# Stick-breaking attention: four query blocks meet the values in one group of products, in six of eight heads

## The chip, the cores and the metric

One core of a Trainium2 chip runs the whole program. The metric is the time of one execution on the device in microseconds (us); each kernel is run several times, and the median counts.

## The reference

A residual block over 1024 tokens of width 1024. Stick-breaking attention with 8 heads of width 64 and an HGRN2 recurrence run side by side on the same normalised input, are gated and merged, and an MLP and a last norm follow. The change is in the attention, which is:

```python
def block(args):
    qi, i = args                      # one block of 128 queries
    qpos = i * Q_BLOCK + jnp.arange(Q_BLOCK)
    z = jnp.einsum('bhqd,bhkd->bhqk', qi, k) * scale
    mask = kpos[None, :] < qpos[:, None]
    log_beta = jax.nn.log_sigmoid(z)
    log_rem = jnp.where(mask, log_beta - z, 0.0)
    between = lax.cumsum(log_rem, axis=3, reverse=True) - log_rem
    w = jnp.where(mask, jnp.exp(log_beta + between), 0.0)
    return jnp.einsum('bhqk,bhkd->bhqd', w, v)
```

A query sees only earlier keys: query block qb needs the key blocks 0 to qb.

## The kernel before

Products run on TensorE (PE) with operands split into a high part and a low remainder (`fp32r` tiles named ...h and ...l), so one exact product is two or three matmuls. `hi_lo` makes such a pair: ACT casts the high part out of the source (line 156), DVE subtracts it from the source for the low part (line 161). All matmuls go through the helper at line 128, all transposes through line 131.

In the attention stage (about 75 to 330 us of the span) the loop at the end of the kernel walks over 64 items, 8 heads times the query blocks in the order 7, 0, 6, 1, 5, 2, 4, 3. At each item it issues

- `weights` for the next item: DVE turns sigmoids into weights by a scan (`rm`, line 826) and a product (`bt`, line 169);
- `scores` for the item after that: PE forms z, ACT takes two sigmoids of each piece (`rm` line 804, `bt` line 807), POOL zeroes one column (line 808);
- some steps of the stream `st`, projections of later heads (`pjqk`, `pjf`, `pjq`, `pga`), which fill TensorE between the attention's own products;
- `turn` for the item itself: PE transposes its weight blocks into a PSUM bank `pw`, and `hi_lo` writes them as `wTh` and `wTl`;
- `values` for a pair of query blocks (2 qc, 2 qc + 1) whose both turns are done: PE multiplies the stationary values by the transposed weights into a bank `po`, ACT copies it to `osb` (line 902), and after a head's last copy two DMAs add its halves and store it. A pair that is complete at one item is multiplied at the next; the last pair of a head falls into the turn of the next head's block 7, between its two groups of transposes.

Products and filling are kept in order on TensorE by hand: `open_block` names the lane, and each block waits in issue order for its lane's last one, a filling block also for an earlier one of the main lane. `after` gives such an order without a wait.

A pair qc has 2 qc + 2 key blocks, each with 256 query columns; where key block 2 qc + 1 meets query block 2 qc there is nothing, and POOL sets those 128 columns to zero (line 862). Tiles come from a pool of 40 slots of 1024 columns (`slot`) and one of 10 halves of 512 columns (`slot_n` up to 512). The weights of pair 0 take two halves, those of pair 1 two slots, of pair 2 two slots and two halves, of pair 3 four slots. `to_come` counts a head's output copies.

Of the kernel before, what the change touches and what calls it, by code (L numbers as in the profile page):

```python
# [9 lines left out]
F32 = mybir.dt.float32  # L10
F32R = mybir.dt.float32r
# [8 lines left out]
P = 128  # L20
T = 1024
D = 1024
NT = T // P
# [16 lines left out]
def kernel(  # L40
# [19 lines left out]
    nc = tc.nc  # L60
# [14 lines left out]
    def slot(name, dt=F32):  # L75
        return spool.tile([P, 1024], dt, tag="s", name=name)

    def slot_n(name, n, dt=F32):

        if n <= 512:  # L80
            return hpool.tile([P, 512], dt, tag="h", name=name)
        return slot(name, dt)

    def bank(name):
        return psum.tile([P, 512], F32, tag="p", name=name)
# [19 lines left out]
    def after(ins, earlier):  # L105
        if earlier is not None and earlier.ins is not ins.ins:
            tc.add_manual_dep(ins.ins, earlier.ins.name, NOSYNC, reason="issue order")
        return ins

    def open_block(name):  # L110
        cur[0] = name
        lane = lanes[name]
        lane.gates = (lane.last,)
        if name == "main":
            lane.ends.append(lane.last)
        else:
            ends = lanes["main"].ends
            lane.gates += tuple(ends[-AHEAD : len(ends) - AHEAD + 1])

    def pe(ins):  # L120
        lane = lanes[cur[0]]
        for g in lane.gates:
            after(ins, g)
        lane.last = ins
        return ins

    def matmul(*a, **k):
        return pe(nc.tensor.matmul(*a, **k))  # L128

    def transpose(dst, src):  # L130
        return pe(nc.tensor.transpose(dst, src, ident))  # L131
# [9 lines left out]
    def lo_now(behind=None):  # L141
        while owed_wlo:
            after(owed_wlo.pop()(), behind)
# [9 lines left out]
    hi_behind, hi_last, turn_hi = [None], [None], [None]  # L153

    def hi_copy(dst, src):
        hi_last[0] = after(in_turn("act", nc.scalar.copy(dst, src)), hi_behind[0])  # L156

    def lo_sub(dst, src, hi):
        return in_turn(
            "dve",  # L160
            nc.vector.tensor_tensor(out=dst, in0=src, in1=hi.bitcast(F32), op=ALU.subtract),  # L161
        )

    def hi_lo(h, l, src):
        hi_copy(h, src)
        return lo_sub(l, src, h)
# [501 lines left out]
    vt, qk, osb = {}, {}, {}  # L668
# [9 lines left out]
    def v_stat(h, tb):  # L678
        c = ((tb % 2) * 4 + h % 4) * P
        return vt[h // 4, tb // 2][:, c : c + P]  # L680
# [101 lines left out]
    zs, wTt, seen = {}, {}, {}  # L782
    lastsel, turn_lo = [None], [None]
# [32 lines left out]
    def weights(h, qb):  # L816
# [7 lines left out]
        for i, (a, b) in enumerate(parts):  # L824
# [14 lines left out]
            if qb == 5:  # L839
                after(m, turn_lo[0])  # L840

    def turn(h, qb, between):

        open_block("main")
        bt, rm = zs.pop((h, qb))
        qc, par = qb // 2, qb % 2
        nkb = 2 * qc + 2
        if (h, qc) not in wTt:
            wTt[h, qc] = [
                tuple(  # L850
                    slot_n(f"wT{n}{h}_{qc}_{k0}", 256 * min(nkb - k0, 4), F32R).rearrange(
                        "p (k q) -> p k q", q=256
                    )
                    for n in "hl"
                )
                for k0 in range(0, nkb, 4)
            ]
        tiles = wTt[h, qc]
        qs = slice(par * P, (par + 1) * P)
        if par == 0:  # L860
            for t in tiles[-1]:
                after(nc.gpsimd.memset(t[:, (nkb - 1) % 4, qs].bitcast(F32), 0.0), lastsel[0])
        order = list(enumerate(tiles))
        for i, (th, tl) in order[::-1] if qb == NT - 1 else order:
            n = min(qb + 1 - 4 * i, 4)
            if n <= 0:
                continue
            if qb == NT - 1 and i == 0:
                between()
                open_block("main")  # L870
            pw = bank(f"pw{h}_{qb}_{i}")
            for kb in range(n):
                s0 = (4 * i + kb) * P
                transpose(pw[:, kb * P : (kb + 1) * P], bt[:, s0 : s0 + P])
            turn_lo[0] = hi_lo(
                th[:, 0:n, qs], tl[:, 0:n, qs], pw[:, : n * P].rearrange("p (k q) -> p k q", q=P)
            )
            turn_hi[0] = hi_last[0]
        lo_now(turn_lo[0])
        seen[h, qc] = seen.get((h, qc), 0) + 1  # L880
        return (h, qc) if seen[h, qc] == 2 else None

    to_come, od = {}, {}

    def values(h, qc):
        open_block("main")
        tiles = wTt.pop((h, qc))
        nkb = 2 * qc + 2
        po = bank(f"po{h}_{qc}")[:, 0:256]
        for kb in range(nkb):  # L890
            for i in range(2):
                matmul(
                    po,
                    v_stat(h, kb),
                    tiles[kb // 4][i][:, kb % 4, :],
                    start=kb == 0 and i == 0,
                    stop=kb == nkb - 1 and i == 1,
                )
        if to_come.get(h) is None:
            to_come[h] = NT // 2  # L900
            osb[h] = slot(f"osb{h}")
        kept = nc.scalar.copy(osb[h][:, qc * 256 : (qc + 1) * 256], po)
        to_come[h] -= 1
        keep_attended(behind=kept)
        if to_come[h] == 0:
            nc.gpsimd.dma_start(osb[h][0:DHS, :], osb[h][DHS:P, :], accum_op=ALU.add)
            summed.append(h)
# [3 lines left out]
    def keep_attended(queue=nc.scalar, behind=None):  # L911
        while summed:
            h = summed.pop()
            pair, r = h // 2, (h % 2) * DHS
            if r == 0:
                od[pair] = dram(f"od{pair}", [P, 1024])
            after(queue.dma_start(od[pair][r : r + DHS, :], osb.pop(h)[0:DHS, :]), behind)
# [1435 lines left out]
    for i, it in enumerate(items):  # L2353
        if i + 1 < len(items):
            weights(*items[i + 1])
        if i + 2 < len(items):
            st.finish(j_qk[items[min(i + 4, len(items) - 1)][0]])
            scores(*items[i + 2])
        if i % 2 == 1:
            next(wsums, None)  # L2360
        want = n_first + (i + 1) * (n_fill - n_first) // len(items)
        st.advance(want - done, j_att)
        done = want
        before = ready.popleft() if ready else None

        def between():
            if before:
                values(*before)

        r = turn(*it, between)  # L2370
        if i == len(items) - 2:
            attended[0] = turn_lo[0]
        if it[1] != NT - 1:
            between()
        if r:
            ready.append(r)
    st.finish(j_att)
    st.advance(1, j_q[2])
    while ready:
        values(*ready.popleft())  # L2380
# [125 lines left out]
```

## Time and profile before

| | |
|---|---|
| median of 3 runs | 1421.49 us (1421.34 to 1421.5) |
| profiled execution | 1421.23 us, its span 1419.4 us |
| granted TensorE clock | 0.999 |
| instructions | 18788 |
| value products (`po`) | 320, all of 256 columns |
| casts of transposed weights (`wTh`) | 96 |

The span is what the profiler saw between the first and the last instruction. "Busy" of TensorE counts overlapping, pipelined matmuls once. In the rows of groups, the numbers behind the bar are the busy time, the mean ns of one, and the idle time of the engine ahead of them with what ended it. In rows by time the first number is the start, the second the length, both in us.

### The profile page before, as it was taken

The page shows a single profiled execution, that of the slowest core. Times are in us where ns is not written, and L with a number is a line of the kernel's source. Part 1 is how long each engine was busy: PE and PEld are TensorE (multiplying, and loading weights), DVE is VectorE, ACT ScalarE, POOL GpSimd, SP SyncE. Part 2 cuts the span into 40 slices and gives each one's busy share as a digit, 9 for nine tenths or more (in the row PEclk, how much of TensorE's full clock was granted, in tenths as well). Part 3 has the DMA queues.
Part 4 walks back from the last instruction along what each step waited for, and adds up shares of the span by engine and source line. Part 5 has one row for each costly group of instructions (what it writes and reads, how often), then busy time and mean ns, then how long its engine had stood idle before and what let it go on. Part 6 is the DMA issues. An engine that isn't in the chain of part 4 may idle for free.

```text
span 1419.4 us, 18788 instructions
## 1 busy us (share of the span) xinstructions
PE 1408.7 (99%) x6848; PEld 1183.7 (83%) x6848; DVE 1087.5 (77%) x1494; ACT 684.5 (48%) x1181; POOL 142.0 (10%) x340
## 2 busy tenths in 40 slices
PE   9999999999999999999999999999999999999998
PEld 8888888888888888888888888888888888888886
DVE  7579988988567888887788897677666657768765
ACT  6356676664243554433244764445444443434343
POOL 3012223210011031000000300000000000000031
PEclk9999999999999999999999999999999999999999
DMA  7124445535135785364585515444446974776824
GB/s 239 29 67 127 104 101 96 106 78 151 65 73 163 233 219 178 130 215 156 158 300 194 185 53 171 163 162 141 140 145 239 354 263 153 279 273 234 281 100 180
DMA packets 162597, 237.72 MB, mean 167 GB/s; under 512 B 26268, under 2 KB 93384, under 8 KB 162504
## 3 DMA queue, kind: packets, MB, share of 16 engines
q1 hardware_dynamic: 145480, 190.37, 40.0%
q0 software_dynamic: 11584, 34.61, 9.9%
q10 hardware_dynamic: 5440, 11.54, 2.3%
q8 instruction: 54, 0.88, 0.2%
q14 instruction: 39, 0.32, 0.1%
HBM read 168.32 MB, written 66.06 MB: 165 GB/s over the span
## 4 chain that ended last, share of the span: by engine, by line
PE 97%; ACT 1%; DVE 1%; POOL 0%; DMA 0%; issue 0%; SPq 0%; DVEq 0%; ACTq 0%
PE pm L128 21%; PE pX L128 9%; PE pW L128 6%; PE pY L128 6%; PE pjqk L128 6%; PE pga L128 4%; PE gX L128 4%; PE gY L128 4%; PE pjf L128 3%; PE pys L128 3%; PE pji L128 3%; PE pyh L128 3%; PE pjq L128 3%; PE pjv L128 3%; PE po L128 3%; PE z L128 2%
## 5 line engine op out<-in xcount | busy, mean ns | idle before, releaser
L156 ACT CAST whid<-w 128x1024 fp32r<-128x1024 f32 x30 | 31.6, 1054 | 154.3 <-PE pm L128 86.0
L826 DVE TENSOR_TENSOR_SCAN rm<-rm,bits 128x511 f32<-128x511 f32 (+7 forms) x72 | 87.4, 1219 | 17.1 <-ACT rm L804 16.8
L128 PE MATMUL pm<-whid,sh 128*128 128x512 f32 x240 | 93.4, 389 | 0.0
L128 PE MATMUL pm<-wlod,sh 128*128 128x512 f32 x240 | 93.4, 389 | 0.0
L128 PE MATMUL pm<-whid,sl 128*128 128x512 f32 x240 | 93.4, 389 | 0.0
L128 PE MATMUL pm<-tl,sh 128*128 128x512 f32 (+1 forms) x210 | 81.3, 387 | 0.0
L128 PE MATMUL pm<-th,sl 128*128 128x512 f32 (+1 forms) x210 | 81.3, 387 | 0.0
L128 PE MATMUL pm<-th,sh 128*128 128x512 f32 (+1 forms) x210 | 81.3, 387 | 0.0
L161 DVE TENSOR_TENSOR wlod<-w,whid 128x1024 fp32r<-128x1024 f32 x30 | 36.6, 1222 | 55.7 <-ACT whid L156 55.7
L161 DVE TENSOR_TENSOR sl<-sa,sh 128x1024 fp32r<-128x1024 f32 x56 | 68.2, 1217 | 0.1
L156 ACT CAST wTh<-pw 128x512 fp32r<-128x512 f32 (+2 forms) x96 | 43.8, 485 | 41.6 <-PE pw L131 40.7
L156 ACT CAST sh<-sa 128x1024 fp32r<-128x1024 f32 x56 | 57.2, 1046 | 7.3 <-DMA sa<-ad 7.3
L2140 POOL TENSOR_SCALAR fss<-fss 128x1 f32<-128x1 f32 x8 | 3.3, 415 | 562.0 <-ACT fsc L2135 561.5
L161 DVE TENSOR_TENSOR wTl<-pw,wTh 128x512 fp32r<-128x512 f32 (+2 forms) x96 | 49.9, 546 | 4.3 <-ACT wTh L156 4.1
L128 PEld LDWEIGHTS pm<-whid,sl 128*128 128x128 f32 x240 | 45.1, 188 | 9.4
L128 PEld LDWEIGHTS pm<-wlod,sh 128*128 128x128 f32 x240 | 45.0, 187 | 9.4
L128 PEld LDWEIGHTS pm<-whid,sh 128*128 128x128 f32 x240 | 45.1, 188 | 9.3
L169 DVE TENSOR_TENSOR bt<-bt,rm 128x511 f32<-128x511 f32 (+7 forms) x72 | 49.0, 684 | 3.4
L804 ACT ACTIVATE rm<-z 128x511 f32<-128x511 f32 (+4 forms) x96 | 48.0, 500 | 5.5 <-PE z L128 2.9
L128 PE MATMUL pX<-sqh,t1l 128*128 128x512 f32 x128 | 49.9, 390 | 0.0
L128 PE MATMUL pX<-sql,t1h 128*128 128x512 f32 x128 | 49.9, 390 | 0.0
L128 PE MATMUL pX<-sqh,t1h 128*128 128x512 f32 x128 | 49.8, 389 | 0.0
(930 smaller groups left out, 4430.5 us busy)
## 6 DMA issues: line engine op xcount, KB each, us to landing
w<-in_w_ff_dram SPq DMA_DIRECT2D x72, 512.0 KB, 5.0
sa<-ad SPq DMA_DIRECT2D x56, 512.0 KB, 6.0
ad<-a SPq DMA_DIRECT2D x32, 256.0 KB, 4.6
ad<-s SPq DMA_DIRECT2D x16, 512.0 KB, 3.3
tw<-in_w_out_dram POOLq DMA_DIRECT2D x24, 256.0 KB, 4.6
pr<-pd SPq DMA_DIRECT2D x10, 512.0 KB, 6.1
x<-in_x_dram SPq DMA_DIRECT2D x8, 512.0 KB, 7.8
xnl<-xnh POOLq DMA_DIRECT2D x8, 512.0 KB, 6.4
```

Of the source, the lines that this page charges most:

```text
L128: return pe(nc.tensor.matmul(*a, **k))
L156: hi_last[0] = after(in_turn("act", nc.scalar.copy(dst, src)), hi_behind[0])
L161: nc.vector.tensor_tensor(out=dst, in0=src, in1=hi.bitcast(F32), op=ALU.subtract),
L169: return nc.vector.tensor_tensor(out=out, in0=a, in1=b, op=ALU.mult)
L804: nc.scalar.activation(rm[:, s0 + c0 - 1 : s0 + m - 1], z[:, c0:m], AF.Sigmoid, scale=-0.125)
L826: sc = nc.vector.tensor_tensor_scan(out=rr, data0=rr, data1=bits[:, 1024 - nk + a : 1024 - nk + b][:, ::-1], initial=rm[:, b : b + 1] if i ...
L2140: nc.gpsimd.tensor_scalar(out=ssq, in0=ssq, scalar1=1.0 / D, scalar2=EPS, op0=ALU.mult, op1=ALU.add)
```

## The change

In heads 0 to 5 the query blocks 0 to 3 no longer form two pairs. Their transposed weights go into one layout over two pairs of tiles: a full slot (high and low) that holds key block 0 for four query blocks (512 columns) and key block 1 for query blocks 1 to 3 (384 columns), and a half tile that holds key blocks 2 and 3, each for query blocks 2 and 3 (256 columns; the 128 columns where key block 3 meets query block 2 are set to zero). `values` then runs once for the four, with 8 products into 512 columns of a bank, at the time of the former second pair, and one copy of 512 columns. Query blocks 2 and 3 write their transposes in two `hi_lo` steps, one for each tile. The other pairs, and heads 6 and 7, are as they were.

```diff
+    def four(h, qb):
+        return h < 6 and qb < 4
+
+    def four_blocks(t, qb, k0, n):
+        step = 256 if k0 else 384
+        return bass.AP(
+            tensor=t.tensor,
+            offset=t.offset + (qb - k0) * P,
+            ap=[list(t.ap[0]), [step, n], [1, P]],
+        )
+
+    def turn_four(h, qb, bt, between):
+        tiles = wTt.setdefault((h, 0), [])
+        if not tiles:
+            tiles.append([slot(f"wT{n}{h}_four", F32R) for n in "hl"])
+        if qb == 2:
+            tiles.append([slot_n(f"wT{n}{h}_last", 512, F32R) for n in "hl"])
+            for t in tiles[1]:
+                after(nc.gpsimd.memset(t[:, 256 : 256 + P].bitcast(F32), 0.0), lastsel[0])
+        pw = bank(f"pw{h}_{qb}")
+        for kb in range(qb + 1):
+            cs = slice(kb * P, (kb + 1) * P)
+            transpose(pw[:, cs], bt[:, cs])
+        for (th, tl), k0 in zip(tiles, (0, 2)):
+            n = min(qb + 1 - k0, 2)
+            if n > 0:
+                src = pw[:, k0 * P : (k0 + n) * P].rearrange("p (k q) -> p k q", q=P)
+                turn_lo[0] = hi_lo(
+                    four_blocks(th, qb, k0, n), four_blocks(tl, qb, k0, n), src
+                )
+                turn_hi[0] = hi_last[0]
+        lo_now(turn_lo[0])
+        seen[h, 0] = seen.get((h, 0), 0) + 1
+        return (h, 0) if seen[h, 0] == 4 else None
+
     def turn(h, qb, between):
...
+        if four(h, qb):
+            return turn_four(h, qb, bt, between)
...
     def values(h, qc):
         open_block("main")
         tiles = wTt.pop((h, qc))
-        nkb = 2 * qc + 2
-        po = bank(f"po{h}_{qc}")[:, 0:256]
+        all_four = qc == 0 and four(h, 0)
+        nkb = 4 if all_four else 2 * qc + 2
+        nq = 512 if all_four else 256
+        po = bank(f"po{h}_{qc}")[:, 0:nq]
         for kb in range(nkb):
             for i in range(2):
+                if all_four:
+                    c0, n = ((0, 512), (512, 384), (0, 256), (256, 256))[kb]
+                    w = tiles[kb // 2][i][:, c0 : c0 + n]
+                else:
+                    n, w = 256, tiles[kb // 4][i][:, kb % 4, :]
                 matmul(
-                    po,
+                    po[:, nq - n : nq],
                     v_stat(h, kb),
-                    tiles[kb // 4][i][:, kb % 4, :],
+                    w,
                     start=kb == 0 and i == 0,
                     stop=kb == nkb - 1 and i == 1,
                 )
         if to_come.get(h) is None:
-            to_come[h] = NT // 2
+            to_come[h] = 3 if four(h, 0) else NT // 2
             osb[h] = slot(f"osb{h}")
-        kept = nc.scalar.copy(osb[h][:, qc * 256 : (qc + 1) * 256], po)
+        kept = nc.scalar.copy(osb[h][:, qc * 256 : qc * 256 + nq], po)
```

## The prediction

> **What bounds the kernel now.** I read the engine totals and the chain of the page first, then the busy time by stretches of the attention stage (84 to 330 us), then what TensorE itself waited for there.
>
> ```profile
> PE 1408.7 (99%) x6848; PEld 1183.7 (83%) x6848; DVE 1087.5 (77%) x1494; ACT 684.5 (48%) x1181; POOL 142.0 (10%) x340
> PE 97%; ACT 1%; DVE 1%; POOL 0%; DMA 0%; issue 0%; SPq 0%; DVEq 0%; ACTq 0%
> ...
> 90.00:120.00 30.00, 29.69 (x173) 25.49 (x172) 28.97 (x41) 20.32 (x48) 8.15 (x28) 1.00 0.51 117
> 120.00:150.00 30.00, 30.00 (x176) 26.11 (x175) 27.03 (x39) 21.31 (x49) 7.24 (x26) 1.00 0.49 127
> 180.00:210.00 30.00, 29.59 (x169) 25.28 (x168) 27.41 (x38) 21.09 (x49) 6.58 (x23) 1.00 0.40 96
> 240.00:270.00 30.00, 30.00 (x175) 26.03 (x174) 28.29 (x40) 20.83 (x49) 8.03 (x25) 1.00 0.56 98
> ...
> PE po L128 <- DVE wTl L161: 0.7, 2, 0.4
> ```
>
> The columns of a stretch are its length, then busy us (and instructions) of PE, weight loads, DVE, ACT and POOL, then the granted clock. TensorE is on 97% of the chain, and in the stage that changes it is busy 30.00 of 30 us in two of these four stretches, at clock 1.00. All that it waited for between 84 and 330 us is 0.7 us, twice for the low half of transposed weights. So a product taken off TensorE here is worth its issue interval, no more. The second number to keep is DVE: 26 to 29 of 30 us. DVE isn't the bound, but it is the engine with the least room, and this change gives it work.
>
> **TensorE: what the products cost.** The durations that the profile gives (0.28 us for 256 columns) overlap, so the interval from start to start counts. The chain merges them:
>
> ```profile
> 96.03 0.47 PE po L128 x4
> 111.99 0.95 PE po L128 x8
> 154.71 2.75 PE pjqk L128 x12
> 250.34 0.47 PE po L128 x4
> 264.83 0.96 PE po L128 x8
> ...
> 139.21 0.33 PE L128 MATMUL z<-KS,QH 128*128 128x384 f32 x1
> 139.38 0.34 PE L128 MATMUL z<-KS,QL 128*128 128x384 f32 x1
> 139.56 0.39 PE L128 MATMUL pjqk<-xnh,wqk3h 128*128 128x512 f32 x1
> ```
>
> The x4 rows are the first pair's products (2 key blocks times high and low), the x8 rows the second pair's, shown for the first head (96 and 112 us) and the sixth (250 and 265 us). 256 columns: 0.95/8 = 0.119 us. 512 columns: 2.75/12 = 0.229 us. 384 columns: the starts at 139.21, 139.38 and 139.56 are 0.17 and 0.18 apart, 0.175 us.
> Before: 12 products of 256, 0.47 + 0.95 = 1.42 to 1.43 us a head. After: twice (0.229 + 0.175 + 2 x 0.119) = 1.28 us. Gain 0.14 to 0.15 us a head, six heads: **0.9 us**. The transposes stay what they are (1 + 2 + 3 + 4 blocks). The first product behind transposes is slower than the following ones whichever it is, so that cost moves and isn't saved.
>
> The Trainium skill, "TensorE: Matmul & The Clock Gate", section "Back-to-back issue gap", gives a sustained spacing for streams of weight load and product of about 81 ns at 128 columns and 131 ns at 512. An estimate by a straight line between those two page figures, 98 ns at 256 and 114 ns at 384, makes it 1.17 us against 0.88 us a head, 1.7 us in all, so some 1419.7 us. The trace disagrees: its 512 columns take 0.229 us.
>
> **ACT and DVE: split copies.** Blocks 2 and 3 of a head now leave PSUM in two pieces, for the two tiles: 384 columns become 256 + 128, 512 become 256 + 256. The four blocks' two output copies of 256 become one of 512.
>
> ```profile
> L156 ACT CAST wTh<-pw 128x512 fp32r<-128x512 f32 x46 | 27.1, 590 | 25.9 <-PE pw L131 25.0 <-ACT bt L807 0.4
> L902 ACT COPY osb<-po 128x256 f32<-128x256 f32 x32 | 12.1, 378 | 19.7 <-PE po L128 17.9 <-DVE g L169 1.8
> L156 ACT CAST wTh<-pw 128x384 fp32r<-128x384 f32 x16 | 7.8, 485 | 4.0 <-PE pw L131 4.0
> L156 ACT CAST wTh<-pw 128x256 fp32r<-128x256 f32 x16 | 6.1, 381 | 4.1 <-PE pw L131 4.1
> L156 ACT CAST wTh<-pw 128x128 fp32r<-128x128 f32 x16 | 4.4, 275 | 7.0 <-PE pw L131 7.0
> L990 ACT COPY qx<-pjq 128x512 f32<-128x512 f32 x4 | 2.5, 629 | 0.0
> ...
> L161 DVE TENSOR_TENSOR wTl<-pw,wTh 128x512 fp32r<-128x512 f32 x46 | 30.7, 678 | 2.8 <-ACT wTh L156 2.7
> L161 DVE TENSOR_TENSOR wTl<-pw,wTh 128x384 fp32r<-128x384 f32 x16 | 8.7, 546 | 0.3 <-ACT wTh L156 0.3
> L161 DVE TENSOR_TENSOR wTl<-pw,wTh 128x256 fp32r<-128x256 f32 x16 | 6.6, 413 | 0.0
> L161 DVE TENSOR_TENSOR wTl<-pw,wTh 128x128 fp32r<-128x128 f32 x16 | 4.5, 281 | 1.2 <-ACT wTh L156 1.1
> ```
>
> ACT a head: 381 + 275 - 485 = 171 ns and 2 x 381 - 590 = 172 ns more for the casts; 2 x 378 - 629 = 127 ns less for the copy (629 ns is the only plain copy of 512 columns quoted here). Net +0.22 us a head, +1.3 us in six heads, with ACT at 20 to 21 of 30 us.
> DVE a head: 413 + 281 - 546 = 148 ns and 2 x 413 - 678 = 148 ns, +0.30 us a head, +1.8 us in six. A head lasts about 31 us, so DVE goes from 27 to 27.3 of 30 where it is typical and from 28.97 to 29.3 around the first head.
> I count both at nothing on the path. The cover is here, in the second head:
>
> ```profile
> 138.51 0.68 DVE L161 TENSOR_TENSOR wTl<-pw,wTh 128x512 fp32r<-128x512 f32 x1
> 140.91 2.02 DVE L826 TENSOR_TENSOR_SCAN rm<-rm,bits 128x895 f32<-128x895 f32 x1 [1.72 <-ACT rm L804]
> ...
> 141.31 0.36 PE L128 MATMUL po<-wTh,V 128*128 128x256 f32 x1
> ```
>
> The low half of the last block's weights ends at 139.2 us, its product starts at 141.31 us, and DVE then stands idle for 1.72 us, waiting for ACT's sigmoids of the next head. An extra 0.3 us of DVE fits into that, and the products that need the second piece (key blocks 2 and 3) now come behind four wider ones, 2 x (0.229 + 0.175) = 0.8 us later in the group. If that cover were gone, the extra 0.30 us of DVE and 0.34 us of casts would show on TensorE; that is a rival below. On the other side, the two waits of 0.7 us could go if the order shifts kindly: bounds of this term are -0.7 and +3.8 us (6 x 0.64); I take 0, since the rows of waits are nearest to it.
>
> **POOL and the memory slots.** Block 0 brought two memsets a head, block 2 two; block 0's go, 12 in all.
>
> ```profile
> L808 POOL MEMSET bt<- 128x1 f32 x60 | 13.4, 256 | 19.8 <-PE po L128 7.4 <-DVE bt L169 5.3 <-DMA od<-osb 3.2
> L862 POOL MEMSET wTl<- 128x128 f32 x32 | 10.6, 409 | 9.8 <-DMA od<-osb 7.8 <-PE po L128 1.3 <-PE pw L131 0.7
> L862 POOL MEMSET wTh<- 128x128 f32 x31 | 10.4, 415 | 8.2 <-PE po L128 7.0 <-DVE bt L169 0.8 <-DMA od<-osb 0.5
> ```
>
> 12 x 0.41 = 4.9 us less of POOL, an engine at 7 to 8 of 30 us: nothing on the path. What these rows do show is that tiles of weights wait for a slot to come free: the one 7.8 us wait is for a store of an earlier head's result, 7.0 us are for value products. Slots are what the change uses more of. The pair of block 0 and 1 lay in two half tiles; now its successor is two full slots of 1024 columns, held from block 0's turn (second of eight) to the end of the head, where before two full slots were taken at block 2's turn (sixth). So in turns 2 to 5 two more of the 40 slots are gone. Counted from the code, while query blocks 7 and 6 are at work: 16 slots of normalised input, 8 of values, 6 of queries and keys (9 where the projections run ahead), 4 of weights of blocks 6 and 7, 3 of scores in work, 1 of results, about 38; with two more, 40. It fits, barely. A wait would come in front of ACT's cast of block 0 or of a score's sigmoid, and behind ACT's queue stand the sigmoids that DVE's scans need.
> Half tiles: two fewer from block 0's turn, two more from block 2's, out of 10; no row shows a wait for one. The one output copy is later for blocks 0 and 1 and not for 2 and 3, so the DMAs of the head's result keep their time. No DMA is added or moved, and no queue gets another order but by these instructions.
>
> **The sum.** The profiled execution took 1421.23 us, of which the span is 1419.4 and 1.83 lie around it; the median of the three runs is 1421.49, 0.26 more. 1421.23 - 0.9 = 1420.3, in a median run 1420.6. About 0.2% (2.8 us) is what a measurement of this kernel can tell from no change.
>
> **The rivals.**
> 1. *The narrow pieces show* (a chance of 0.11). For: DVE is at 28.97 and 28.29 of 30 us in two stretches, and once TensorE waited for exactly such a low half. Against: the 1.72 us of idle DVE a head. All of ACT's and DVE's extra on the path is 6 x (0.34 + 0.30) = 3.8 us, less 0.9: 1424.4 us; half of it, 1422.5. The Trainium skill, "VectorE: DVE Perf Modes", section "The TRN2 errata — SBUF-src ops pay a fixed extra latency per instruction", speaks against the change in the same way: one large tile pays that latency once, many small ones each pay it; the rows above agree for these reads, with 148 ns for each piece more.
> 2. *Slots run out, slower* (0.18). A cast of the new tile, or a score's sigmoid, waits for a slot in ACT's queue, the low half behind it is late on DVE, and TensorE waits for it. What TensorE then shows is seen here:
>
> ```profile
> 182.10 0.40 PE L128 MATMUL pjqk<-xnl,wqk5h 128*128 128x512 f32 x1
> 182.34 0.39 PE L128 MATMUL pjqk<-xnh,wqk5l 128*128 128x512 f32 x1
> 183.14 0.39 PE L128 MATMUL po<-wTl,V 128*128 128x256 f32 x1 [0.41 <-DVE wTl L161]
> ```
>
> The start at 182.34 is followed by one at 183.14: 0.80 us where 0.23 is usual, a hole of 0.57 us. One such hole a head gives 3.4 - 0.9, 1424.0 us. It decides the sign from 0.15 us a head, and passes 0.2% from (2.8 + 0.9)/6 = 0.62 us a head; two holes a head give 6.8 - 0.9 = 5.9, 1427.4 us. I give one hole a head 0.04 and two 0.14. For: 38 of 40 slots. Against: before has waits for slots on POOL, and none of them is among TensorE's.
> 3. *The gain is given back* (0.08): the earlier scores meet the same ACT and DVE queue, and the 0.9 us returns as waits: 1421.5 us.
> 4. *Far more is gained* (0.06): the 0.7 us of waits here go, and a shift in order also cures part of TensorE's idle time elsewhere, 10.7 us in all (1419.4 - 1408.7): 1418.5 us or less.
> That the change doesn't do what it says I give nothing: 24 products go, by the code.
>
> **How the numbers follow.** Forecast 0.57, 1420.6 us. Same within 0.2%: forecast, rival 3, most of rival 1 and one hole a head of rival 2, 0.57 + 0.08 + 0.09 + 0.04 = 0.78. Slower: two holes a head and the top of rival 1, 0.14 + 0.02 = 0.16. Faster: rival 4, 0.06. The range 1419.1 to 1424.4 holds all but rival 4 and two holes a head, 0.80; its lower end is the forecast with both waits gone and as much again for holes too short to be listed as waits, 1420.6 - 0.7 - 0.8, its upper end rival 1 in full.
>
> **What would show it.** Right: between 84 and 330 us, value products in groups of 8 (1.28 us) in the first six heads and no groups of 4 there; 296 value products in place of 320; casts of wTh 108 in place of 96; output copies 26 in place of 32; TensorE's own waits in this stage still under 1 us; the stage after it shifted earlier by about 0.9 us. Wrong: waits of TensorE for DVE wTl or bt, or holes between its starts, once in each of the first six heads (rivals 1 and 2; in rival 2 ACT's casts or sigmoids wait for a value product or a scan), or a 512-column value product that takes longer than 0.23 us.

## The result and the profile after

The changed kernel takes 1424.63 us in the median, the kernel before 1421.4 us in the runs beside it: a ratio of 1.0023, interval 1.0016 to 1.0031. It is 3.2 us slower where 0.9 us less was forecast. The profiled execution has a span of 1422.8 us, 3.4 us more than before. Of all executions on record, one, in experiment 5, took 3064.8 us; the ratio there is without it.

Three views follow: the chain by engine, the stretches of the attention stage (length, then busy us and instructions of PE, weight loads, DVE, ACT and POOL, then the granted clock, the share of busy DMA and GB/s), and what TensorE, ACT and DVE waited for between 84 and 335 us (us in all, times, the longest).

```profile
PE 89%; DVE 2%; ACT 0%; DMA 0%; issue 0%; POOL 0%; DVEq 0%; ACTq 0%
...
90.00:120.00 30.00, 28.18 (x155) 23.55 (x154) 28.02 (x42) 19.30 (x46) 6.99 (x23) 1.00 0.45 104
120.00:150.00 30.00, 30.00 (x174) 25.95 (x173) 26.89 (x38) 21.17 (x50) 7.79 (x26) 1.00 0.47 128
180.00:210.00 30.00, 30.00 (x170) 25.49 (x169) 27.35 (x39) 21.67 (x50) 7.27 (x26) 1.00 0.44 104
240.00:270.00 30.00, 28.95 (x165) 24.73 (x164) 26.92 (x41) 20.38 (x48) 5.57 (x20) 1.00 0.54 97
...
PE po L128 <- DVE wTl L161: 1.9, 5, 0.6
PE po L128 <- DVE wTl_last L161: 0.7, 1, 0.7
PE po L128 <- ACT wTh L156: 0.5, 1, 0.5
...
ACT wTh_last L156 <- DVE wTl_four L161: 7.4, 7, 1.6
...
DVE wTl L161 <- DMA od<-osb: 1.2, 1, 1.2
```

The chain of the changed kernel could be followed back only to 104.30 us of the span, so its 89% can't be set beside the 97% of before; the stretches and the waits can.

The work on TensorE did shrink as forecast: 296 value products, 108 casts of transposed weights, 26 output copies. The group of the second head, in order of time (start, length):

```profile
142.75 0.48 PE L128 MATMUL po<-wTh_four,V 128*128 128x512 f32 x1
143.07 0.39 PE L128 MATMUL po<-wTl_four,V 128*128 128x512 f32 x1
143.30 0.34 PE L128 MATMUL po<-wTh_four,V 128*128 128x384 f32 x1
143.48 0.35 PE L128 MATMUL po<-wTl_four,V 128*128 128x384 f32 x1
143.66 0.28 PE L128 MATMUL po<-wTh_last,V 128*128 128x256 f32 x1
...
144.13 0.60 PE L131 MATMUL pw<-ident,bt 128*128 128x128 f32 x4
```

From the first start to the next transposes are 1.38 us. The first product stands 0.09 us longer than the others of its width, as behind transposes before; without that it is 1.29 us, where the prediction has 1.28. The intervals of 0.23, 0.18 and 0.12 us are those that the sum used.

The loss is in the first and last of the four stretches: TensorE is busy 28.18 and 28.95 of 30 us where it was 29.69 and 30.00. Its waits rise from 0.7 to 3.1 us. By the distance of its starts, less the usual distance of the same two shapes, the gaps over 0.15 us in the stage are these: before 0.57 us (182 us), 0.47 (91) and 0.24 (106), 1.3 us in all; after 0.47 (91), 0.75 and 0.61 (105 and 106), 0.83 (113), 0.49 (168), 0.72 (246) and 0.74 (261), 4.6 us in all. So 3.3 us more, of which 0.9 comes back in shorter groups: 2.4 us. From the same product at its start (83.80 us before, 83.73 after) to the first `pji` product behind it (339.69 and 342.63 us) the stage is 3.0 us longer, so about 0.6 us are spread over it in less than 0.15 us each, and the last 0.4 us of the 3.4 lie behind it. No run here assigns these 1.0 us.

Two waits are new in kind. The second cast of a block, into `wTh_last`, waits for DVE's first subtraction of the same block, 7 times. And DVE once waits 1.2 us for the store of an earlier head's result.

### The profile page after: what moved, and what is told of

Read it like the earlier page. It is cut to its first block, busy times and chain, and to the rows that moved or that the text cites. A ratio compares the mean times of both kernels' runs of the same rounds, so it can differ in the third digit from the quotient of the medians.

```text
span 1422.8 us, 18717 instructions
## 1 busy us (share of the span) xinstructions
PE 1409.7 (99%) x6824; PEld 1182.3 (83%) x6824; DVE 1088.3 (76%) x1506; ACT 684.4 (48%) x1187; POOL 145.6 (10%) x328
## 4 chain that ended last, share of the span: by engine, by line
PE 89%; DVE 2%; ACT 0%; DMA 0%; issue 0%; POOL 0%; DVEq 0%; ACTq 0%
PE pm L128 21%; PE pX L128 9%; PE pW L128 6%; PE pY L128 6%; PE gX L128 4%; PE gY L128 4%; PE pjqk L128 4%; PE pga L128 4%; PE pys L128 3%; PE pji L128 3%; PE pyh L128 3%; PE pjq L128 3%; PE po L128 2%; PE pwX L128 2%; PE pjf L128 2%; PE pgq L128 2%
## 5 line engine op out<-in xcount | busy, mean ns | idle before, releaser
L807 ACT ACTIVATE bt<-z 128x512 f32<-128x512 f32 (+3 forms) x96 | 48.0, 501 | 0.6 <-PE pgq L128 0.6
L128 PEld LDWEIGHTS pm<-th,sh 128*128 128x128 f32 x210 | 39.4, 188 | 8.1
```

What stands on the lines that cost most here:

```text
L807: nc.scalar.activation(bt[:, s0 : s0 + e], z[:, :e], AF.Sigmoid, scale=0.125)
```

## The experiments

Three theories stood against each other. **W**: the two-step copy makes ACT wait for DVE between its two casts. **M**: two more slots are held, and something waits for a slot. **S**: the first pair's products leave their place in turn 5, and what is around them no longer fits together. All times below are medians; a ratio is to the kernel before in the runs beside it, 1421.4 to 1421.5 us. Gaps are read from one profiled execution of each kernel, and some of these lie above the median: 1424.31 us in experiment 1, 1427.22 in experiment 6, 1423.81 in experiment 12. Gaps of before that stay are not named each time.

**1. Casts first.** In the turns of blocks 2 and 3 both casts are issued ahead of both subtractions.

```diff
+                hi_copy(h_, src)
+                parts.append((l_, src, h_))
+        for l_, src, h_ in parts:
+            turn_lo[0] = lo_sub(l_, src, h_)
```

> The change, but in the turns of blocks 2 and 3 ACT's two casts are issued ahead of DVE's two subtractions, so the second cast no longer waits for the first subtraction (in the change it does: 7.4 us of ACT's idle time, 7 times). Theory W (that wait is what the change lost): the 7.4 us are gone, TensorE's waits in the attention stage fall from 3.1 to about 1 us, and the time is 1420.5 to 1421.5. Theory M (slots): the second cast's wait did not matter, the time stays at 1424 to 1425. Theory S (the first pair's products leave turn 5, TensorE arrives earlier and waits for weights that come no sooner): 1423.5 to 1425, with the holes at the third pair's products as in the change.

Measured: 1423.1 us, ratio 1.0016 (1.0007 to 1.0025). ACT's wait for the first subtraction is gone, and 1.5 us with it, but 1.7 us stay. W is a part and not the whole. Left are gaps of 0.90 us (105 us), 0.69 (167), 0.71 (244) and 2.04 (260); the last belongs to an execution 1.2 us above the median.

**2. Two banks.** Key blocks 2 and 3 get a bank of their own, cast and subtraction in the order of the change.

```diff
-        pw = bank(f"pw{h}_{qb}")
+        pws = [bank(f"pw{h}_{qb}_{i}") for i in range(qb // 2 + 1)]
...
```

> The change, but key blocks 2 and 3 are transposed into a PSUM bank of their own, so neither engine waits for the other over a shared bank. Theory W: as with the casts first, 1420.5 to 1421.5, a little worse if the 8 banks get short. Theories M and S: 1423.5 to 1425.

Measured: 1423.21 us, ratio 1.0015 (1.0006 to 1.0023), the same as with the casts first, and the same four gaps (the last 0.75 us here, in a profiled execution of 1422.90 us). So what W needs is the shared bank: with two banks no cast waits for a subtraction, in the same order of casts and subtractions as in the change.

**3. The split alone.** The kernel before, blocks 2 and 3 of heads 0 to 5 copied in two steps.

```diff
+            cuts = ((0, 2), (2, n)) if h < 6 and qc == 1 else ((0, n),)
+            for a, b in cuts:
+                turn_lo[0] = hi_lo(
...
```

> The kernel before, with one edit: in heads 0 to 5 the transposes of blocks 2 and 3 leave PSUM in two steps (key blocks 0 and 1, then the others), cast, subtraction, cast, subtraction as in the change; tiles, slots and products are those of before. Theory W: the second cast waits for DVE as in the change, 1423 to 1425 (the change's loss without TensorE's gain of 0.9 us would be up to 1425.5). Theories M and S: DVE's 1.8 us extra at most, 1421.4 to 1422.

Measured: 1423.2 us, ratio 1.0013 (1.0004 to 1.0022). The split costs 1.8 us in the kernel before, with a gap of 1.19 us at 112 us and one of 0.42 us at 204 us, both inside second pairs. ACT waits for DVE's subtractions as in the change, here under the old tile names:

```profile
ACT wTh L156 <- DVE wTl L161: 4.6, 6, 1.1
```

**4. The new tiles with the old products.** The change's slots and split, but pairs of 256 columns at their old times.

```diff
-            ap=[list(t.ap[0]), [step, n], [1, P]],
+            ap=[list(t.ap[0]), [256, n], [1, P]],
...
-        return (h, 0) if seen[h, 0] == 4 else None
+        return {2: (h, 0), 4: (h, 1)}.get(seen[h, 0])
```

> The tiles and the split steps of the change (a full slot from block 0's turn to the end of the head, a half for key blocks 2 and 3), but the products of before: two pairs of 256 columns at their old times, two copies, two memsets a head more. Theory W: as the split alone, 1423 to 1425.5. Theory M: 1424 to 1426, the change without its gain, while the split alone is near 1421.5. Theory S: the first pair's products are back in turn 5, so near 1421.5 to 1422.

Measured: 1424.14 us, ratio 1.0019 (1.001 to 1.0028), 0.9 us more than the split alone. Beside that one's gaps (1.18 and 0.43 us) stand 0.46 and 0.98 us at 260 and 261 us, and DVE waits for a store (ACT too, once, for 1.8 us near 159 us, where TensorE shows no gap). The gaps at 167 and 244 us aren't there, and the one of before at 182 us is gone.

```profile
DVE wTl L161 <- DMA od<-osb: 2.3, 1, 2.3
```

**5. The first pair late.** The kernel before, with the first pair's products issued at the end of the head.

```diff
+        if r and r[0] < 6 and r[1] == 0:
+            held = r
+        elif r and r[0] < 6 and r[1] == 1:
+            ready.append((held, r))
...
```

> The kernel before, with one edit: in heads 0 to 5 the first pair's four products (0.47 us) are issued together with the second pair's at the end of the head, where the change has its group. Tiles, slots, casts and products are those of before. Theory S (the 0.47 us in turn 5 gave the weights of blocks 4 and 5 time that DVE needs; TensorE arrives earlier and waits): holes of 0.4 to 0.9 us appear in front of the third pair's products near 105 and 167 us, as in the kernels with the change, and the time is 1422.4 to 1423.5. Theory M or W alone: no such holes, 1421.2 to 1421.7.

Measured: 1422.57 us, ratio 1.0007 (0.9998 to 1.0016). The interval takes in 1, but the lowest of these runs, 1422.28, lies above the highest of the kernel before beside them, 1421.67. The gaps are where S puts them, 0.70 us at 105.65 and 0.80 us at 166.87. They have two causes. Near 105 us DVE's order is that of before. First the kernel before, then this one:

```profile
105.66 0.88 DVE L161 TENSOR_TENSOR wTl<-pw,wTh 128x512 fp32r<-128x512 f32 x2
106.04 0.36 PE L128 MATMUL po<-wTh,V 128*128 128x256 f32 x1
```

```profile
105.73 0.88 DVE L161 TENSOR_TENSOR wTl<-pw,wTh 128x512 fp32r<-128x512 f32 x2
105.65 0.36 PE L128 MATMUL po<-wTh,V 128*128 128x256 f32 x1
106.47 0.38 PE L128 MATMUL po<-wTl,V 128*128 128x256 f32 x1 [0.45 <-DVE wTl L161]
```

The low half starts at 105.66 and 105.73 us, and TensorE comes to it 0.39 us sooner than before (0.62 us sooner in the casts-first kernel, at 105.42 us); so the time that the moved products left goes by idle, and the products are still to be done at the end of the head. Near 167 us it is DVE's order. Again DVE in the kernel before, then this kernel:

```profile
164.30 1.21 DVE L161 TENSOR_TENSOR wqk5l<-wqk5r,wqk5h 128x1024 fp32r<-128x1024 f32 x1
165.43 0.87 DVE L161 TENSOR_TENSOR wTl<-pw,wTh 128x512 fp32r<-128x512 f32 x2
166.23 1.51 DVE L826 TENSOR_TENSOR_SCAN rm<-rm,bits 128x511 f32<-128x511 f32 x2
```

```profile
163.99 1.21 DVE L826 TENSOR_TENSOR_SCAN rm<-rm,bits 128x511 f32<-128x511 f32 x1
165.30 0.69 DVE L169 TENSOR_TENSOR bt<-bt,rm 128x511 f32<-128x511 f32 x1
165.91 1.22 DVE L161 TENSOR_TENSOR wqk5l<-wqk5r,wqk5h 128x1024 fp32r<-128x1024 f32 x1
167.05 0.88 DVE L161 TENSOR_TENSOR wTl<-pw,wTh 128x512 fp32r<-128x512 f32 x2
...
166.87 0.36 PE L128 MATMUL po<-wTh,V 128*128 128x256 f32 x1
167.78 0.39 PE L128 MATMUL po<-wTl,V 128*128 128x256 f32 x1 [0.55 <-DVE wTl L161]
```

A scan and a product of the next head now stand ahead of the low half that TensorE needs next, which so starts at 167.05 and not at 165.43 us. The changed kernel has the same order there, with one more subtraction in between. Why DVE's order changes when four products move, no run here shows.

**6. Filling ahead.** Casts first, and one step of filling moved into turns 5, 2 and 4.

```diff
+        want += it[0] < 6 and i % 8 in (4, 5, 6)
```

> The casts-first version of the change, with one more filling step (6 products, 1.4 us) issued by turn 5, 2 and 4 of the first six heads, and one fewer after them. Theory S: TensorE has work where the first pair's products were, the holes near 105 and 166 us go or shrink, and the time falls from 1423.1 to 1421 to 1422, the rest being the wait for a slot in the sixth head. Theory M or W alone: 1423 or more.

Measured: 1426.04 us, ratio 1.0033 (1.0021 to 1.0046), worse by 2.9 us than casts first. The gap at 105 us stays (0.30 and 0.61 us), and TensorE gets new ones, 1.0 us in two gaps near 200 us and one at 166 us, this time for the weights themselves:

```profile
166.21 0.40 PE L128 MATMUL pjq<-xnh,wq0l 128*128 128x512 f32 x1
168.08 0.44 PE L131 MATMUL pw<-ident,bt 128*128 128x128 f32 x2 [1.47 <-DVE bt L169]
```

The expectation was wrong: a filling step is 1.4 us where 0.5 us was missing, and what comes with it on ACT and DVE was not counted. It speaks neither for nor against S.

**7. Five heads.** Casts first, heads 0 to 4.

```diff
-        return h < 6 and qb < 4
+        return h < 5 and qb < 4
```

> The casts-first version for heads 0 to 4 only. Theory M (in the sixth head the two longer-held slots make a weight tile wait for the store of an earlier head's result, 1 to 2.3 us): that wait and the hole near 260 us go, 1422.2 to 1422.6, at a cost of 0.15 us of gain. Theory S alone: the hole near 260 us stays or its place is taken by one in another head, 1423.

Measured: 1421.9 us, ratio 1.0003 (0.9994 to 1.0012), 1.2 us below six heads. The gaps at 244 and 260 us and DVE's wait for a store are gone; those at 105 (0.90 us) and 167 us (0.70 us) stay.

**8. Five heads and filling ahead.** The edits of 6 and 7 together.

> Casts first, one filling step ahead, heads 0 to 4 only. If S, M and W are all there are, every loss is gone and five heads' gain of 0.15 us stays: 1420.3 to 1421.3. If something else is lost as well, 1421.5 to 1423.

Measured: 1424.0 us, ratio 1.0018 (1.0009 to 1.0026). That is above both ranges of the expectation. As in 6, the filling brings gaps of its own, 1.63 us at 166 us and 1.0 us near 200 us.

**9. Heads 1, 3 and 4.** Casts first, without the two heads of S and the one of M.

```diff
-        return h < 6 and qb < 4
+        return h in (1, 3, 4) and qb < 4
```

> Casts first, the four blocks in one group in heads 1, 3 and 4 alone: left out are heads 0 and 2, where TensorE waits for DVE in front of the third pair's products, and head 5, where a slot is waited for. Theory S with W and M (the losses belong to those heads): no new hole, three heads' gain of 0.15 us, 1420.4 to 1421.2, below the kernel before by 0.2 to 1.0 us. If the holes only move to the heads that still have the group: 1421.6 to 1422.5.

Measured: 1420.51 us, ratio 0.9993 (0.9984 to 1.0002). The interval reaches just over 1; the runs don't overlap (1420.18 to 1420.69 against 1420.93 to 1421.92). No new gap: 0.48 us at 91 and 0.25 us at 106 us are those of before, and the one of 0.57 us at 182 us is gone. Three heads' 0.15 us and that gap are 1.0 us, and 0.9 us are measured. In the same stretches TensorE is busy again:

```profile
90.00:120.00 30.00, 29.68 (x173) 25.48 (x172) 28.99 (x41) 20.42 (x48) 7.86 (x26) 1.00 0.50 117
240.00:270.00 30.00, 30.00 (x173) 25.96 (x172) 27.83 (x40) 20.82 (x48) 8.05 (x25) 1.00 0.57 99
```

Why the gap at 182 us goes isn't settled. It goes wherever head 3 has the new tiles, in experiment 4 too, and stays where head 3 has the tiles of before, whether its copies (3, 11) or the times of its products (5) are changed or not.

**10. Five heads, copies as in the change.** Experiment 7 with cast, subtraction, cast, subtraction.

> The change as it is (cast, subtraction, cast, subtraction) in heads 0 to 4 only; it differs from the five heads with the casts first (1421.9 us) in that order alone, and no head waits for a slot. Theory W: 0.8 to 1.6 us more, 1422.7 to 1423.5, with the hole near 113 us in front of the second piece's low half, and the second cast's wait for DVE in ACT's row. If the slot wait was the whole of the change's loss besides S: 1421.9 to 1422.2.

Measured: 1423.08 us, ratio 1.0011 (1.0002 to 1.0021), 1.2 us above experiment 7. The gap of 0.83 us at 113 us is back. DVE, ACT and TensorE of the changed kernel at that place, where experiment 10 has the same rows 0.1 us later:

```profile
110.84 0.41 DVE L161 TENSOR_TENSOR wTl_four<-pw,wTh_four 128x256 fp32r<-128x256 f32 x1
...
111.82 2.02 DVE L826 TENSOR_TENSOR_SCAN rm<-rm,bits 128x895 f32<-128x895 f32 x1
113.75 0.40 DVE L161 TENSOR_TENSOR wTl_last<-pw,wTh_last 128x256 fp32r<-128x256 f32 x1
...
111.28 0.37 ACT L156 CAST wTh_last<-pw 128x256 fp32r<-128x256 f32 x1 [0.67 <-DVE wTl_four L161]
...
113.26 0.28 PE L128 MATMUL po<-wTh_last,V 128*128 128x256 f32 x1
114.20 0.38 PE L128 MATMUL po<-wTl_last,V 128*128 128x256 f32 x1 [0.67 <-DVE wTl_last L161]
```

ACT's second cast starts when DVE has done the first subtraction (110.84 + 0.41 = 111.25 us). It ends at 111.65 us. But in DVE's order the next head's work now stands between the two subtractions, last a scan of 2.02 us that starts at 111.82 us, so the second subtraction comes only at 113.75 us. What TensorE loses here is this place in DVE's order; no run keeps the wait and changes the order alone.

**11. The split alone, casts first.** Experiment 3 without the wait.

```diff
...
+            for a, b in cuts:
+                hi_copy(th[:, a:b, qs], pq[:, a:b])
+            for a, b in cuts:
+                turn_lo[0] = lo_sub(tl[:, a:b, qs], pq[:, a:b], th[:, a:b, qs])
```

> The kernel before with the transposes of blocks 2 and 3 of heads 0 to 5 leaving PSUM in two steps, as in the split alone (1423.2 us), but with both casts ahead of both subtractions. It has the 24 more pieces and not the wait. Theory W: 1421.3 to 1421.9. If the pieces' own time on DVE and ACT (0.30 and 0.34 us a head) is what costs: 1422.5 to 1423.3, as the split alone.

Measured: 1421.53 us, ratio 1.0 (0.9992 to 1.0009). The 24 more pieces cost nothing; the order cast, subtraction, cast, subtraction is the whole of the split's 1.7 us. DVE at the place of experiment 10 has both subtractions in a row again, ahead of the next head's scans:

```profile
110.48 0.74 DVE L161 TENSOR_TENSOR wTl<-pw,wTh 128x256 fp32r<-128x256 f32 x2
111.14 2.32 DVE L826 TENSOR_TENSOR_SCAN rm<-rm,bits 128x127 f32<-128x127 f32 x2
```

**12. Head 5 alone.** Casts first, the sixth head only.

> Casts first, the four blocks in one group in the sixth head (number 5) alone. Theory M (the two longer-held slots make a weight tile of its third pair wait for the store of the head before): DVE waits 1 to 2.3 us for that store, a hole of 0.7 to 2 us near 260 us and the one near 244 us appear, and the time is 1422 to 1423.3. If the losses of that head come from the heads ahead of it: 1421.2 to 1421.6, no wait for a store.

Measured: 1423.2 us, ratio 1.0014 (1.0005 to 1.0023). One head loses 1.7 us. The profiled execution, 0.6 us above that, has gaps of 0.78 us at 244 and 1.71 us at 260 us. DVE and TensorE:

```profile
251.66 0.55 DVE L984 TENSOR_SCALAR pp<-pp,oml,lb 128x512 f32<-128x512 f32 x1
254.26 1.02 DVE L161 TENSOR_TENSOR wTl<-pw,wTh 128x512 fp32r<-128x512 f32 x2 [2.06 <-DMA od<-osb]
...
259.50 0.40 PE L128 MATMUL pjf<-xnh,wf1h 128*128 128x512 f32 x1
261.44 0.39 PE L128 MATMUL po<-wTl,V 128*128 128x256 f32 x1 [1.54 <-DVE wTl L161]
```

The low half of the third pair's weights can't be written until head 4's result is stored from the slot that it gets; all of DVE stands for 2.06 us, and five microseconds later TensorE does. In the changed kernel's chain that store has a row of its own:

```profile
248.88 6.11 DMA od<-osb
```

The store was no shorter before. In the kernel before, POOL's zeros for a weight tile wait for the same store, and neither DVE nor TensorE stands still there:

```profile
254.39 0.21 POOL L862 MEMSET wTl<- 128x128 f32 x1 [7.78 <-DMA od<-osb]
```

With the two slots held longer, the slot goes to a tile that DVE has to write at once. The length of the gap follows the store: in experiments 1 and 2 it is issued at 247.36 and 247.28 us, DVE gets its slot at 254.70 and 253.33 us, and the gaps are 2.04 and 0.75 us.

The gap at 244 us comes with it, though not by a wait: ACT takes a cast of the keys (239.14 us) ahead of the sigmoids that it took first before (239.07 us), and the scan behind them starts at 241.21 instead of 240.46 us. The slots alone don't make it: experiment 4 holds them in the same way and has no such gap, and neither has experiment 5, with the moved products alone. Its cause stays open. With it the store is issued 0.8 us later (247.27 us, before 246.45), so part of the gap at 260 us may come from it.

## Why the prediction was wrong, point by point

**TensorE's gain** was right in mechanism and size: the group's intervals are the row's. Experiment 9's 0.9 us fit it for three heads, but only 0.45 us of them are this gain; the other half is the gap at 182 us, which nobody forecast. The sustained spacing of 131 ns at 512 columns that the Trainium skill gives in "TensorE: Matmul & The Clock Gate", section "Back-to-back issue gap", is not met: here too the starts are 0.23 us apart.

**"I count both at nothing on the path"** is the step that failed, though not for the reason that rival 1 gave. The time of the added pieces costs nothing (experiment 11, ratio 1.0). What I didn't see is that two steps through one bank add a wait of ACT for DVE: in cast, subtraction, cast, subtraction the second cast waits for the first subtraction (7.4 us in all), and the second subtraction loses its place in DVE's order, in the first head to a scan of 2.02 us. Its cost: 1.5 us in the change (against casts first), 1.2 us in five heads, 1.7 us in the kernel before. The Trainium skill gives the rule behind it in "PSUM — Partial Sum Buffer", section "PSUM bank collisions raise a hardware error": two engines must not be in the same bank and partitions at once, reads against reads included, so software orders them. The traces agree: the wait is there with one bank (the change, experiment 3) and gone with two (experiment 2).

**The cover** was read from one place, the second head, where DVE stood idle for 1.72 us. In the first head the same step had no such cover, as the 28.97 of 30 us there could have told: I used that row for an average and not for that place.

**What the moved products leave behind** wasn't costed. I counted the first pair's 0.47 us in turn 5 as gain alone. Moving them, with everything else as before, costs 1.1 us (experiment 5): once because TensorE only comes earlier to weights that aren't ready, once because DVE's order changed. Rival 3, "The gain is given back", had the first of these at 0.9 us in all; the second I did not have.

**The slots**, rival 2, were right as a mechanism and wrong in place and number. I had one or two holes a head, in ACT's queue; it is one head of six, in DVE's queue, and that head costs 1.2 us in the casts-first kernel (experiments 1 and 7) and 1.7 us alone (experiment 12), the open gap at 244 us included. What I held against it, that the waits for slots are POOL's and none is TensorE's, was true of the kernel before; the 7.8 us row was the wait for that store, and the change moved it to DVE.

**The sum**, with the costs as measured one by one: -0.9 for TensorE, +1.2 to 1.5 for the wait between the casts, +1.35 for head 5 (1.2 and the 0.15 of its gain, which is in the first term), +1.1 for the moved products, -0.57 for the gap at 182 us, makes 2.2 to 2.5 us. The measured loss is 3.2 us. The single costs were taken in kernels with different neighbours and need not add; the remaining 0.7 to 1.0 us are not assigned.

**The range** ended at 1424.4 us, the result is 1424.63. It took rival 1 in full and left out the case that came, several of the rivals at once: I had laid them side by side as alternatives.

## What to carry to other kernels

When one copy out of a PSUM bank becomes two, issue both reads of one engine before those of the other, or use two banks; otherwise the second read waits for the other engine, and on that engine other work can get ahead of the last step (1.2 to 1.7 us here). When products are moved away, look at what was running beside them: if the engine that feeds TensorE has no room at that place, TensorE stands still there. When a kernel has the same step in many heads, try it head by head: with the group of four in heads 1, 3 and 4 the kernel takes 1420.51 us, a gain at the edge of what the runs can tell, with heads 0 and 2 as well 1421.9 us, and with head 5 too 1423.1 us.

## What was not expected of the hardware

A store that is in nobody's way can come onto the chain: the 256 KB store of head 4's result stands there for 6.11 us, because a tile that DVE writes at once got its slot; before, the same store kept only POOL waiting, for 7.78 us. And this kernel's time moves with the order of one engine's queue: in experiment 5 a scan and a product ahead of a low half on DVE make a gap of 0.80 us on TensorE, as much as the products of five heads can save.
